# A two-layer diffusion backbone: when weight bounds are taken, and three stretches of the context's feed-forward in a written order

## The chip, the cores and the metric

The kernel runs on one core of a Trainium2 chip. The metric is the device time of one execution in microseconds (us), as the median of several runs. The core's engines are TensorE (PE, matrix products; its weight loads are listed as PEld), VectorE (DVE), ScalarE (ACT) and GpSimd (POOL); SyncE (SP) and POOL issue most of the transfers (DMA) between memory and the on-chip buffers. Each engine works through its own queue of instructions in the order in which they were put there.

## The reference

Two layers work on 1024 latent tokens and 256 context tokens of width 1024. Layer 0 mixes with Fourier groups and a Hyena convolution, layer 1 with neighbourhood attention; each ends with a SwiGLU feed-forward of width 2816. Cut to what the change touches:

```python
def rms_norm(x, g):
    y = x32 * lax.rsqrt(jnp.mean(x32 * x32, axis=-1, keepdims=True) + RMS_EPS)
    return (y * g).astype(x.dtype)
...
h_lat = h_lat + g1 * y_lat                                   # y = mixer(...) @ w_out
h_lat = h_lat + g2 * swiglu(modulate(rms_norm(h_lat, norm2_g[i]), sh2, sc2), w_gate, w_up, w_down)
if not last:
    h_ctx = h_ctx + cg1 * y_ctx
    h_ctx = h_ctx + cg2 * swiglu(modulate(rms_norm(h_ctx, norm2_g[i]), csh2, csc2), w_gate, w_up, w_down)
```

`swiglu(u)` is `(silu(u @ w_gate) * (u @ w_up)) @ w_down`, and `modulate` is `h * (1 + scale) + shift`. Layer 1 needs the context's result only as keys and values, so layer 0 is the only one with a feed-forward for the context.

## The kernel before

**Numbers.** Activations stand transposed: channels on the 128 partitions, tokens along the rows. `pc` names a part of the tokens: 0 and 1 are the two halves of the latent tokens (512 each), 2 is the context (256). Channels come in `KB = 8` blocks of 128, the feed-forward's width in `NFB = 22`. Each operand is split in a high and a low part (`split`: a copy on ACT, L301, and a difference on DVE, L303), and each product is three matmuls: high by high, high by low, low by high. `lin` makes the 24 matmuls of one output block over eight input blocks.

**Order.** The program is traced in the order of the text, and a scheduler then puts each engine's instructions in a queue, by their priority (their place in the text) and by a timing model. `follow` binds an instruction behind another one of its engine. Inside a `manual_schedule` region the named engines keep the order of the text instead; where the region's instructions fall among others stays the scheduler's choice. Before the change such regions exist in the attention and at the start of layer 1's feed-forward.

**The stages that the change touches, in order of time.**

- `out_proj` (L1192): the output projection of layer 0, in two groups of eight blocks: first `pc` 2 and 0 together, then `pc` 1. Each block's weight is split one block ahead. After a product DVE adds it to the residual (L1211), ACT squares the result (L510) and DVE adds up the squares (L515). One step of `qkv_sums` runs in each block.
- `qkv_sums` (L1269): 44 tiles of layer 1's and layer 0's weights (512 KB each, loaded from POOL's queue) are read for bounds of their size: ACT takes the absolute values and sums them (`abs_sums`, L1266). A step is three tiles.
- `after1` (L2362, in `run`), after each group: it stores the residual; after the first group it also computes the norm of the two parts. `rms_begin` sums the squares over the partitions on PE (one column per 128 tokens) and takes the root on ACT; `rms_end` scales an identity on ACT (L539), spreads it on PE, and ACT copies it back. `norm_block` makes the context's operand `uf`, `operand_scale` and `first_scales` the scales, and `wino_first` the upper half's operands for the latent product. After the second group only the norm of `pc` 1 is computed.
- `ffn` (L1515) with `l = 0`: for each of 22 blocks it loads and splits a gate and an up weight (`pair3`: three pairs of buffers in turn), makes the two products for the context, applies Silu on ACT (L1553), multiplies on DVE (L1554) and stores the hidden rows. From the third block on, each block also makes one of the 20 steps of `wino_second`: scaled operands (L1372), differences (L1378), a cast on ACT (L1363) and a low part on DVE (L1364).
- The latent gate and up follow as Strassen-like products (`wino_steps`, L1463): seven products for each pair of blocks, with `snap` (L1478) copying an accumulator out on ACT. `fetch(i, m)` loads and prepares the weights of pair `i`; for all but the first pair of a layer it first takes their bound with `abs_sums`.
- `down` (L1668): seven passes for the latent tokens, then (L1778 to L1810) the context's down product: 22 blocks of 24 matmuls into four accumulators. The splits of the weights use two pairs of buffers (`pair1`). `after(1)` (that is `after2` in `run`, L2384) normalizes `pc` 1 for layer 1 with `norm_half` (L569 on DVE, L571 on ACT, L572 on DVE) while it runs, at the calls of `hook`.
- Layer 1 begins with `values`. `halves_ahead` prepares layer-1 weights (L1232 on ACT, L1233 on DVE); the scheduler may put it into gaps of the context's down product.

Of the kernel before, what the change touches and what calls it, by code (L numbers as in the profile page):

```python
# [19 lines left out]
P = 128  # L20
# [181 lines left out]
class Builder:  # L202
# [359 lines left out]
    def norm_half(self, x, b, pc, act, r, cols):  # L562

        nc = self.nc
        w = WID[pc]
        cols = cols[1 if pc == 2 else 0]
        sh, sc = cols[:, b:b + 1], cols[:, 8 + b:9 + b]
        t = self.T()
        nc.vector.scalar_tensor_tensor(t[:, :w], x, sc, r[:, :w], op0=MUL, op1=MUL)  # L569
        hi, lo = act.ap(0, b, pc), act.ap(1, b, pc)  # L570
        nc.scalar.activation(hi, t[:, :w], AF.Identity, bias=sh)  # L571
        nc.vector.scalar_tensor_tensor(lo, t[:, :w], sh, hi, op0=ADD, op1=SUB)  # L572
# [619 lines left out]
    def out_proj(self, wname, y, groups, h, l, m, after, fill):  # L1192
        nc, a = self.nc, self.a
        todo = [nb for pcs in groups for nb in range(KB)]
        ready = []

        def fetch():
            if todo:
                ready.append(self.weights(a[wname][todo.pop(0)]))

        fetch()
        for pcs in groups:
            for nb in range(KB):
                wh, wl = ready.pop(0)
                fetch()
                acc = self.lin(wh, wl, 0, range(KB), y, pcs)
                next(fill, None)
                for pc in pcs:
                    w = WID[pc]
                    t = h.ap(0, nb, pc)  # L1210
                    nc.vector.scalar_tensor_tensor(t, acc[pc][:, :w], self.ada_col(l, pc, m, nb), t, op0=MUL, op1=ADD)  # L1211
                    self.square(t, nb, pc)
            after(pcs)
# [55 lines left out]
    def qkv_sums(self):  # L1269
# [7 lines left out]
        for j, k in enumerate((32, 33, 34, 35, *range(32), *range(36, 44))):  # L1277
# [3 lines left out]
            if j % 3 == 2:  # L1281
                yield
        yield
# [68 lines left out]
    def wino_second(self, h, l, m, r):  # L1352
# [8 lines left out]
        def out(key, j, src):  # L1361
# [3 lines left out]
            if l == 0 or len(late) > 1:  # L1365
                late.pop(0)()
# [96 lines left out]
    def wino_steps(self, w, tile, ctile=None):  # L1463
# [12 lines left out]
        def snap(ps, tile=tile):  # L1476
            t = tile()
            nc.scalar.copy(t, ps)  # L1478
            return t
# [35 lines left out]
    def ffn(self, l, u, h, hs, second, after, keep=None, begun={}):  # L1515
# [28 lines left out]
        if u is not None:  # L1544
            for fb in range(NFB):
                wide = 3 if fb < NFB - 2 else 2
                gh, gl = self.weights(a["gate"][l, fb], wide=wide)
                uh, ul = self.weights(a["up"][l, fb], wide=wide)
                lo = self.last_lo
                ga = self.lin(gh, gl, 0, range(KB), u, (2,))[2]  # L1550
                ua = self.lin(uh, ul, 0, range(KB), u, (2,))[2]
                t = self.T()
                nc.scalar.activation(t[:, :256], ga[:, :256], AF.Silu)  # L1553
                nc.vector.tensor_tensor(t[:, :256], ua[:, :256], t[:, :256], MUL)  # L1554
                self.ldr(hidc[fb // 2][:, fb % 2], t[:, :256])
                if fb >= 2:
                    with self.follow(last):
                        next(second, None)
                last = lo
# [31 lines left out]
        for i in range(n2):  # L1591
# [29 lines left out]
            if i or not begun:  # L1621
                fetch(i + 1, 0)
            g.to(5)
            up.to(1)
# [43 lines left out]
    def down(self, l, scales, bops, sops, hidc, hs, h, todo, after, keep):  # L1668
# [109 lines left out]
        if l == 0:  # L1778
# [4 lines left out]
            for kb in range(NFB):  # L1783
                hook(kb)
                if kb in (4, 8, 12, 16):
                    load_h((kb // 2 - 2, kb // 2 - 1), 2)
                t = self.S2(F32R)
                f = t[:, 256:].bitcast(F32)
                with self.follow(self.last_ldr):
                    self.ldr(f, hidc[kb // 2][:, kb % 2])  # L1790
                self.split(f, t[:, :256], t[:, 256:])
                f = self.pw.tile([P, 1024], F32, tag="ws", name=self.nm("ws")) if kb % 3 < 2 else self.S4()
                wh, wl = self.pair1()
                self.ld(f.rearrange("p (r k) -> p r k", r=2), w[kb].rearrange("r p k -> p r k"))
                self.split(f, wh, wl)
                for nb in range(KB):

                    o = acc[nb // 2][:, nb % 2 * 256:nb % 2 * 256 + 256]
                    with self.follow(end):
# [4 lines left out]
                    end = m.ins  # L1804
# [396 lines left out]
    def run(self):  # L2201
# [158 lines left out]
        rest = []  # L2360

        def after1(pcs):  # L2362
            spill(h, hs0, pcs)
            if 0 in pcs:
                uf.t.update(self.new_act(pcs=(2,)).t)
                rs = self.rms(pcs)
                for b in range(KB):
                    self.norm_block({b: h.ap(0, b, 2)}, b, 2, 0, 3, uf, rs[0])
                load_h((1,))
                self.ucol, self.usi = self.operand_scale(0, 3, (0, 1))  # L2370
                self.first_scales(0)
                for _ in self.wino_first(h, 0, 3, rs[1]):
                    pass
            else:
                rest.append(self.rms((1,))[0])

        load_h((2, 0))
        self.out_proj("w_out", y, [(2, 0), (1,)], h, 0, 2, after1, self.qkv_sums())
# [5 lines left out]
        def after2(pc):  # L2384
# [3 lines left out]
            yield  # L2388
            for b in range(KB):
                if b % 2 == 0:  # L2390
                    self.new_half(u1, ((b, pc), (b + 1, pc)))
                self.norm_half(h3.ap(0, b, pc), b, pc, u1, r, self.u1col)
                if b % 2:
                    yield

        h3 = Act()
        self.ffn(0, uf, h3, hs0, (x for r in rest for x in self.wino_second(h, 0, 3, r)), after2, hd)
# [210 lines left out]
```

## Time and profile before

| | |
|---|---|
| median of 3 runs | 2876.33 us (2871.45 to 2881.31) |
| the profiled execution's own time | 2880.55 us |
| its span, first to last instruction | 2878.8 us |
| mean granted clock of PE | 0.981 |
| output projection, first group | products from 722.3 to 789.9 us |
| second group | 796.0 to 843.2 |
| context's gate and up | 848.9 to 978.6 |
| context's down (but 12 products at 1587) | 1600.7 to 1668.8 |

The page of the profile gives, for each engine, the busy time over the span; the windows give the same for any stretch, with PEclk, the clock that the throttle granted to PE, as a share of full speed. The timeline lists instructions in order; a bracket holds the idle time in front of one and what ended it. A group of instructions has its count, busy time and mean duration. Matmuls overlap, so the pace of a row of products is read from their starts, not from their durations.

### The profile page before, as it was taken

What the parts mean: (1) busy time and instruction counts of PE and PEld (TensorE: products, weight loads), DVE (VectorE), ACT (ScalarE), POOL (GpSimd) and SP (SyncE); (2) the same over time, 40 slices, a digit from 0 to 9 for tenths busy, and PEclk for the clock granted to TensorE, in tenths of its full rate; (3) what the DMA queues carried; (4) which work ended last, traced back from release to release, by engine and by line L of the source; (5) the groups of instructions that cost most, each with busy time, mean ns of one, the idle gap of its engine ahead of it and who ended that gap; (6) DMA issues with size and microseconds to landing.
All of it is one profiled execution on the core that took longest, in us unless ns stands there. A gap on an engine that the chain in (4) does not pass through costs nothing. (4 is left out here: it accounts for less than half of the span.)

```text
span 2878.8 us, 46360 instructions
## 1 busy us (share of the span) xinstructions
PE 2751.2 (96%) x16419; PEld 1684.7 (59%) x16419; DVE 2082.7 (72%) x3857; ACT 1620.5 (56%) x2857; POOL 594.4 (21%) x977
## 2 busy tenths in 40 slices
PE   6989999999999999999999899999999999999998
PEld 3766556878879744444455754666665444444554
DVE  4778867585367798886886877777775788775755
ACT  4674324454575666664555555666663486564543
POOL 1012013264220111122111112333431022102001
PEclk8899999999999999999999999999999999999999
DMA  7574435358785655565996599778775676425653
GB/s 257 190 263 164 167 119 156 104 177 262 288 330 211 216 211 198 198 208 191 330 323 242 206 345 347 173 167 177 162 201 174 231 262 226 146 92 187 225 198 122
DMA packets 323363, 607.60 MB, mean 211 GB/s; under 512 B 89910, under 2 KB 131576, under 8 KB 323130
## 3 DMA queue, kind: packets, MB, share of 16 engines
q1 hardware_dynamic: 254682, 387.53, 42.0%
q0 software_dynamic: 66144, 212.91, 21.0%
q10 hardware_dynamic: 2304, 4.20, 0.4%
q8 instruction: 129, 2.11, 0.3%
q14 instruction: 104, 0.85, 0.1%
HBM read 455.33 MB, written 135.53 MB: 205 GB/s over the span
## 5 line engine op out<-in xcount | busy, mean ns | idle before, releaser
L1473 PE MATMUL ps<-s,s 128*128 128x512 f16 x2244 | 506.1, 381 | 9.5 <-ACT g L1478 5.2
L1473 PEld LDWEIGHTS <-s 128*128 128x128 f16 x2640 | 257.9, 98 | 324.8 <-issue 18.0
L297 PE MATMUL ps<-s,wh 128*128 128x256 f32 (+3 forms) x1716 | 387.0, 329 | 11.1 <-ACT wh L301 5.4
L1232 ACT ACTIVATE s<-s,c 128x512 f16<-128x512 f32 (+1 forms) x324 | 233.1, 752 | 151.5 <-DMA s<-d 86.9
L1233 DVE SCALAR_TENSOR_TENSOR s<-s,c,s 128x512 f16<-128x512 f32 (+1 forms) x324 | 248.2, 793 | 91.8 <-ACT s L1232 91.2
L1698 PE MATMUL ps<-s 128*128 128x512 f16 (+2 forms) x1308 | 303.6, 378 | 2.0 <-DVE s L1233 2.0
L297 PE MATMUL pq<-s,wh 128*128 128x512 f16 (+1 forms) x940 | 259.2, 352 | 2.0 <-ACT wh L1232 1.7
L297 PE MATMUL ps<-s,wl 128*128 128x256 f32 (+3 forms) x858 | 254.6, 330 | 1.3 <-DVE wl L303 1.2
L1698 PEld LDWEIGHTS <-s 128*128 128x128 f16 x1536 | 148.4, 98 | 179.0 <-issue 6.8
L297 PEld LDWEIGHTS <-wh 128*128 128x128 f16 x1568 | 149.8, 99 | 138.1 <-issue 12.5
L288 POOL DMA_DIRECT2D d<-s x201 | 109.1, 543 | 580.5 <-DVE s L1233 159.8
L349 ACT CAST mat<-cs 128x1024 fp32r<-128x1024 f16 (+2 forms) x120 | 111.6, 935 | 140.1 <-PE ps L297 55.9
L297 PEld LDWEIGHTS ps<-s,wh 128*128 128x128 f32 x1088 | 177.7, 192 | 18.1 <-ACT wh L301 5.7
L297 PE MATMUL ps<-s,mat 128*128 128x512 f32 x696 | 180.9, 406 | 4.7 <-DVE s L303 4.4
L1473 PE MATMUL ps<-s,wh 128*128 128x512 f16 x608 | 182.4, 379 | 1.6 <-DVE g L1487 1.2
L297 PE MATMUL pq<-s,wl 128*128 128x512 f16 (+1 forms) x470 | 162.9, 352 | 0.0
L297 PEld LDWEIGHTS <-s 128*128 128x128 f16 x2400 | 113.4, 98 | 80.0 <-issue 10.2
L297 PEld LDWEIGHTS ps<-s,mat 128*128 128x128 f32 x696 | 133.6, 194 | 39.0 <-DVE s L303 5.6
L1266 ACT ACTIVATE t<-s 128x1024 bf16<-128x1024 f32 (+1 forms) x164 | 141.3, 863 | 12.1 <-DVE c L484 8.6
L297 PE MATMUL sc<-s,s 128*128 128x65 f16 (+3 forms) x2688 | 143.2, 231 | 3.3 <-ACT t L2106 2.4
L1232 ACT ACTIVATE s<-t,c 128x512 f16<-128x512 f32 x172 | 115.3, 711 | 22.6 <-DVE c L1333 9.3
L1233 DVE SCALAR_TENSOR_TENSOR s<-t,c,s 128x512 f16<-128x512 f32 x172 | 123.4, 745 | 1.6 <-ACT s L1232 1.6
(438 smaller groups left out, 5504.6 us busy)
## 6 DMA issues: line engine op xcount, KB each, us to landing
s<-d SPq DMA_DIRECT2D x294, 256.0 KB, 4.3
d<-s POOLq DMA_DIRECT2D x157, 256.0 KB, 3.2
s<-in_down SPq DMA_DIRECT2D x154, 256.0 KB, 4.9
s<-in_ada_w POOLq DMA_DIRECT2D x48, 512.0 KB, 4.9
s<-in_gate SPq DMA_DIRECT2D x46, 512.0 KB, 3.8
s<-in_up SPq DMA_DIRECT2D x46, 512.0 KB, 4.2
d<-g POOLq DMA_DIRECT2D x87, 256.0 KB, 3.2
d<-tk POOLq DMA_DIRECT2D x82, 256.0 KB, 4.7
```

The source lines that it names most:

```text
L288: self.last_ldr = self.nc.gpsimd.dma_start(out, in_).ins
L297: return self.nc.tensor.matmul(o, l, r, start=st, stop=sp).ins
L349: self.nc.scalar.copy(m, st)
L1232: nc.scalar.activation(hi, src, AF.Copy, scale=scale)
L1233: nc.vector.scalar_tensor_tensor(lo, src, scale, hi, op0=MUL, op1=SUB)
L1266: self.nc.scalar.activation(junk[:, :t.shape[1]], t, AF.Abs, scale=2.0 ** -15, accum_out=st[:, k:k + 1])
L1473: nc.tensor.matmul(ps, x[:, sl], y, start=first and j == 0 and x is wh and y is xh, stop=j == 3 and x is wl, skip_group_check=True)
L1698: m = nc.tensor.matmul(acc[j][:, c0:c1], x[:, sl], y[:, xs], start=first and k == 0, stop=last and k == 2, skip_group_check=True)
```

## The change

The bounds (`qkv_sums`) take one tile a step instead of three. In the first group of `out_proj` each block runs three steps, in the second one, and 12 of the 44 tiles are left for `ffn`, one in each block from the third on. The norm of the first group moves from the boundary between the groups to behind the first product of the second group (`norm1`). The norm of `pc` 1 and the first scales move into `ffn` (`second1`). The gate and up loop and the context's down loop of `ffn` and `down` are written out with loads ahead (four weights there, two here), splits ahead (two products, one block) and a `manual_schedule` region for PE, ACT and DVE. `fetch(1, 0)` moves behind the fifth step of the first latent gate product, and its bound behind the last `snap`. In `wino_second` a low part is always made one step after its cast. For `pc` 1 `after2` scales on ACT and multiplies by the norm on GpSimd, and the rest of `norm_half` follows one step later.

```diff
     def out_proj(self, wname, y, groups, h, l, m, after, norm, fill):
...
-        for pcs in groups:
+        for g, pcs in enumerate(groups):
             for nb in range(KB):
                 wh, wl = ready.pop(0)
                 fetch()
                 acc = self.lin(wh, wl, 0, range(KB), y, pcs)
-                next(fill, None)
+                if g and nb == 0:
+                    norm(groups[g - 1])
+                for _ in range(1 if g else 3):
+                    next(fill, None)
...
             self.abs_sums([t], self.qs[:, k:k + 1])
-            if j % 3 == 2:
-                yield
-        yield
+            yield
...
             late.append(lambda: nc.vector.tensor_tensor(lo, src, hi, SUB))
-            if l == 0 or len(late) > 1:
+            if len(late) > 1:
                 late.pop(0)()
...
+            def part(k):
+                stage(k + 4)
+                if k < 2 * NFB:
+                    ready[k] = self.pair3() if k // 2 < NFB - 2 else self.pair1()
+                    self.split(staged.pop(k), *ready[k])
+
+            def hidden(fb):
+                ga, ua, t = pending.pop(fb)
                 nc.vector.tensor_tensor(t[:, :256], ua[:, :256], t[:, :256], MUL)
                 self.ldr(hidc[fb // 2][:, fb % 2], t[:, :256])
...
+            with self.tc.manual_schedule(engines={e.PE, e.Activation, e.DVE}):
+                part(0)
+                part(1)
+                for fb in range(NFB):
+                    ga = self.lin(*ready.pop(2 * fb), 0, range(KB), u, (2,))[2]
+                    if fb == 0:
+                        next(second)
+                    else:
+                        hidden(fb - 1)
+                    part(2 * fb + 2)
+                    ua = self.lin(*ready.pop(2 * fb + 1), 0, range(KB), u, (2,))[2]
+                    if fb == 0:
+                        next(second)
+                    t = self.T()
+                    nc.scalar.activation(t[:, :256], ga[:, :256], AF.Silu)
+                    pending[fb] = ga, ua, t
+                    if fb >= 2:
                         next(second, None)
-                last = lo
+                        next(fill, None)
+                    part(2 * fb + 3)
+                hidden(NFB - 1)
...
-            if i or not begun:
+            if i:
                 fetch(i + 1, 0)
             g.to(5)
+            if i == 0 and not begun:
+                self.behind = self.last_snap
+                fetch(1, 0)
             up.to(1)
...
+            def part(kb):
+                stage(kb + 2)
+                if kb < NFB:
+                    t, f, x = staged.pop(kb)
+                    ready[kb] = t, *self.pair1()
+                    self.split(x, *ready[kb][1:])
+                    self.split(f, t[:, :256], t[:, 256:])
...
+            with self.tc.manual_schedule(engines={e.PE, e.Activation, e.DVE}):
+                part(0)
+                for kb in range(NFB):
+                    part(kb + 1)
+                    t, wh, wl = ready.pop(kb)
+                    for nb in range(KB):
...
+                    if kb % 2 or kb == 2:
+                        next(done, None)
...
+        def second1():
+            c = self.rms_begin(1)
+            yield
+            r = self.rms_end(1, c)
+            yield
+            self.first_scales(0)
+            yield from self.wino_second(h, 0, 3, r)
...
+                if pc == 1:
+                    t = self.T()
+                    nc.scalar.mul(t, h3.ap(0, b, pc), self.u1col[0][:, 8 + b:9 + b])
+                    nc.gpsimd.tensor_tensor(t, t, r, MUL)
+                    late.append((t, b))
+                    if b:
+                        self.shift_half(*late.pop(0), pc, u1, self.u1col)
+                    yield
+                    continue
```

More of the change, by code (lines that the diff above doesn't have):

```diff
@@ L1189, in fourier_c, with out_proj @@
             self.split(raws[g][:, :256], y.ap(0, g, 2), y.ap(1, g, 2))
-    def out_proj(self, wname, y, groups, h, l, m, after, fill):
+    def out_proj(self, wname, y, groups, h, l, m, after, norm, fill):
         nc, a = self.nc, self.a
@@ L1513, in wino_begin, with ffn @@
         return s
-    def ffn(self, l, u, h, hs, second, after, keep=None, begun={}):
+    def ffn(self, l, u, h, hs, second, after, keep=None, begun={}, fill=()):
         nc, a = self.nc, self.a
@@ L1544, in ffn @@
         if u is not None:
[L1545 to L1553, printed above, removed]
+            staged, ready, pending = {}, {}, {}
@@ L1555, in ffn @@
                 self.ldr(hidc[fb // 2][:, fb % 2], t[:, :256])
-                if fb >= 2:
-                    with self.follow(last):
-                        next(second, None)
-                last = lo
+            for k in range(4):
+                stage(k)
+            e = mybir.EngineType
+            with self.tc.manual_schedule(engines={e.PE, e.Activation, e.DVE}):
[15 more added lines that the diff above has]
+                    if fb >= 2:
+                        next(second, None)
+                        next(fill, None)
+                    part(2 * fb + 3)
+                hidden(NFB - 1)
@@ L1560, in ffn @@
+            for _ in fill:
+                pass
             self.load_cond()
@@ L1782, in down, with stage @@
             acc = [self.PP() for _ in range(4)]
[L1783 to L1799, printed above, removed]
+            staged, ready = {}, {}
+            def stage(kb):
+                if kb < NFB:
+                    if kb in (4, 8, 12, 16):
+                        load_h((kb // 2 - 2, kb // 2 - 1), 2)
+                    t = self.S2(F32R)
+                    f = t[:, 256:].bitcast(F32)
+                    with self.follow(self.last_ldr):
+                        self.ldr(f, hidc[kb // 2][:, kb % 2])
+                    x = self.pw.tile([P, 1024], F32, tag="ws", name=self.nm("ws")) if kb % 3 < 2 else self.S4()
+                    self.ld(x.rearrange("p (r k) -> p r k", r=2), w[kb].rearrange("r p k -> p r k"))
+                    staged[kb] = t, f, x
+            def part(kb):
+                stage(kb + 2)
+                if kb < NFB:
+                    t, f, x = staged.pop(kb)
+                    ready[kb] = t, *self.pair1()
+                    self.split(x, *ready[kb][1:])
+                    self.split(f, t[:, :256], t[:, 256:])
+            stage(0)
+            stage(1)
+            e = mybir.EngineType
+            with self.tc.manual_schedule(engines={e.PE, e.Activation, e.DVE}):
[4 more added lines that the diff above has]
+                    for nb in range(KB):
+                        o = acc[nb // 2][:, nb % 2 * 256:nb % 2 * 256 + 256]
                         for k, (x, c) in enumerate(((wh, 0), (wh, 256), (wl, 0))):
@@ L2364, in after1, with norm1 @@
             if 0 in pcs:
[L2365 to L2368, printed above, removed]
                 load_h((1,))
[L2370 to L2375, printed above, removed]
+        def norm1(pcs):
+            uf.t.update(self.new_act(pcs=(2,)).t)
+            rs = self.rms(pcs)
+            for b in range(KB):
+                self.norm_block({b: h.ap(0, b, 2)}, b, 2, 0, 3, uf, rs[0])
+            self.ucol, self.usi = self.operand_scale(0, 3, (0, 1))
+            for _ in self.wino_first(h, 0, 3, rs[1]):
+                pass
+        def second1():
[5 more added lines that the diff above has]
+            yield from self.wino_second(h, 0, 3, r)
         load_h((2, 0))
[L2378 removed]
+        sums = self.qkv_sums()
+        self.out_proj("w_out", y, [(2, 0), (1,)], h, 0, 2, after1, norm1, sums)
         for b in range(8):
@@ L2394, in after2 @@
                     yield
+            for t, b in late:
+                self.shift_half(t, b, pc, u1, self.u1col)
+                yield
         h3 = Act()
-        self.ffn(0, uf, h3, hs0, (x for r in rest for x in self.wino_second(h, 0, 3, r)), after2, hd)
+        self.ffn(0, uf, h3, hs0, second1(), after2, hd, fill=sums)
         for b in range(8):
```

15 lines of the change are left out of this document (12 added, 3 removed).

## The prediction

> **What bounds the kernel now.** I read the page first, then windows of 10 us, then TensorE's (PE's) timeline for the rows that carry an idle time.
>
> ```profile
> PE 2751.2 (96%) x16419; PEld 1684.7 (59%) x16419; DVE 2082.7 (72%) x3857; ACT 1620.5 (56%) x2857; POOL 594.4 (21%) x977
> ```
>
> PE is the bound: it is busy for 96% of the span, so 4%, some 115 us, are idle in all. The change can win only the part of it in its own stages, and what a low clock costs there. Windows; the columns are the stretch, its length, the busy times of PE, PEld, DVE, ACT and POOL, then PEclk, DMA share and GB/s:
>
> ```profile
> 790.00:800.00 10.00, 7.61 (x26) 6.44 (x27) 6.62 (x19) 7.33 (x17) 1.08 (x2) 0.66 0.76 256
> ...
> 840.00:850.00 10.00, 5.08 (x24) 3.76 (x23) 2.80 (x4) 7.21 (x15) 2.19 (x4) 0.85 1.03 419
> ...
> 870.00:880.00 10.00, 6.97 (x44) 6.77 (x45) 8.50 (x11) 5.75 (x8) 0.54 (x1) 0.83 0.76 273
> 880.00:890.00 10.00, 10.00 (x90) 10.00 (x90) 8.26 (x13) 5.87 (x8) 1.08 (x2) 1.00 0.43 142
> ```
>
> There are holes at 790 and from 840 to 880, where the granted clock is 0.66 to 0.85, and a steady stretch from 880 on. Two more places are the seam at 990 and the context's down product after 1600. PE's timeline at the first three:
>
> ```profile
> 789.41 0.50 PE L297 MATMUL ps<-s,wl 128*128 128x256 f32 x2
> 792.39 2.66 PE L297 MATMUL pq<-c,tk 128*128 128x1 f32 x12 [2.48 <-DVE tk L515]
> 794.91 1.20 PE L297 MATMUL pq<-t,c 128*128 128x256 f32 x2
> ...
> 795.98 1.20 PE L297 MATMUL ps<-s,wh 128*128 128x512 f32 x2
> ...
> 799.67 0.64 PE L297 MATMUL ps<-s,wh 128*128 128x512 f32 x2
> ...
> 806.12 0.63 PE L297 MATMUL ps<-s,wh 128*128 128x512 f32 x2
> ...
> 806.82 0.62 PE L297 MATMUL ps<-s,wh 128*128 128x512 f32 x2
> ...
> 845.47 1.05 PE L297 MATMUL pq<-c,tk 128*128 128x1 f32 x8 [2.23 <-DVE tk L515]
> 848.85 0.79 PE L297 MATMUL ps<-s,wh 128*128 128x256 f32 x2 [2.32 <-ACT wh L301]
> ...
> 872.27 0.51 PE L297 MATMUL ps<-s,wh 128*128 128x256 f32 x2 [3.07 <-ACT wh L301]
> ...
> 976.06 0.39 PE L297 MATMUL ps<-s,wh 128*128 128x256 f32 x2
> ...
> 976.40 0.39 PE L297 MATMUL ps<-s,wh 128*128 128x256 f32 x2
> ...
> 978.32 0.28 PE L297 MATMUL ps<-s,wl 128*128 128x256 f32 x1
> ...
> 990.92 4.20 PE L1473 MATMUL ps<-s,s 128*128 128x512 f16 x12 [2.86 <-ACT g L1478]
> ```
>
> The reader is to see who is late. At 792 and 845 PE stands before the norm's column sums, which need the last square (DVE L515). At 848 and 872 it stands before a weight's high half (ACT L301), at 990 before an eviction (ACT L1478). Two paces serve below: three 512-wide products start every 806.82 - 806.12 = 0.70 us, and three 256-wide ones every 976.40 - 976.06 = 0.34 us, so 24 of these, one block of gate, up or down, take 2.72 us.
>
> **1. Sums a block later.** Between the end of the first group (789.41 + 0.50 = 789.91) and 795.98 lie 6.1 us. The column sums and the spread of the inverse root stay PE's work wherever they stand: 12 at the pace of the 8 that took 1.05 is 1.6 us, the spread some 0.6. Removed are 6.1 - 2.2 = 3.9 us, because 24 products of the next block now stand first and the squares are done behind them; that block's weights were split a block ahead. From 795.98 to 799.67 nine products took 3.7 us instead of 2.1, at the low clock; with no hole this 1.6 goes too. Together 5.5. Behind the moved step eight normalized context blocks and the upper half's operands start 5 us later, under some 40 us of products that cover them. I take **-5** (bounds 0 and -5.5).
>
> **2. The context's gate and up in a written order.** Here is where it may cost as much as it wins. The stretch of before runs from the end of the second group, where DVE's L1211 stops waiting, to 978.6:
>
> ```profile
> 843.27 0.75 DVE L1211 SCALAR_TENSOR_TENSOR s<-ps,c,s 128x512 f32<-128x512 f32 x1 [3.41 <-PE ps L297]
> ```
>
> That is 135.4 us. PE's work in it is 44 x 2.72 = 119.7, plus about 2 for the sums and the spread: 121.7. So 13.7 us are lost now, all of it before 880. Part of the cause is ACT, which takes weight bounds (L1266) between the splits. The change leaves 12 of the 44 bounds for this loop, one in each of blocks 2 to 13, splits two products ahead, and puts the second norm after the first gate product. The loads keep their queues: the weights on SP, four ahead, the bounds' tiles on POOL, now among the stores of the hidden rows; rival (c) prices a late one. The holes at 845 and 848 should close. But now ACT and DVE issue strictly in the order of the text. Durations (groups by form of 722 to 990, and one row of DVE's timeline):
>
> ```profile
> L303 DVE TENSOR_TENSOR wl<-s,wh 128x1024 fp32r<-128x1024 f32 x44 | 53.7, 1225 | 31.8 <-ACT wh L301 31.8
> ...
> L1266 ACT ACTIVATE t<-s 128x1024 bf16<-128x1024 f32 x45 | 47.0, 1044 | 1.7 <-DMA s<-in_gate 1.7
> L301 ACT CAST wh<-s 128x1024 fp32r<-128x1024 f32 x44 | 45.8, 1048 | 39.6 <-issue 26.3 <-PE ps L297 13.1
> ...
> L1363 ACT CAST s<-s 128x512 f16<-128x512 f32 x16 | 9.9, 616 | 6.4 <-DVE s L1378 5.3 <-DVE s L1386 0.9
> L1554 DVE TENSOR_TENSOR t<-ps,t 128x256 f32<-128x256 f32 x22 | 9.2, 420 | 5.0 <-ACT t L1553 4.4 <-PE ps L297 0.6
> ...
> L1372 DVE SCALAR_TENSOR_TENSOR s<-s,c,t 128x512 f32<-128x512 f32 x8 | 5.9, 747 | 1.8 <-ACT t L543 1.8
> ...
> L1378 DVE TENSOR_TENSOR s<-s,s 128x512 f32<-128x512 f32 x4 | 2.7, 683 | 0.0
> ```
> ```profile
> 852.58 2.36 DVE L303 TENSOR_TENSOR wl<-s,wh 128x1024 fp32r<-128x1024 f32 x2 [2.53 <-ACT wh L301]
> ```
>
> Follow one block, from ACT's cast of an up weight to the next block's: cast 1.05; on DVE the low half 1.23, the hidden product 0.42, the next low half 1.23, the scaled operand 0.75 and the difference 0.68; back on ACT the operand's cast 0.62 and the bound 1.04. The sum is 7.0 us. Rows back to back overlap by about 0.09 (two low halves in 2.36, not 2.45), which makes it 6.7. PE wants a block every 5.44. Behind the waiting operand cast stand, on ACT, the bound and the next weight's cast, and PE waits for that weight. So 1.25 us a block are lost in the eight blocks whose step has both DVE operations (2 to 9), and about 0.6 in the four with one (10 to 13): 10 + 2.4. The start adds two waits. In block 0 ACT does the root, the four scalings, a copy and a table load before the weight of block 1: 1.6. In block 2 the first bounds' reduction passes through PE, so DVE's step begins only when the up product ends, and the next up weight is some 3 late. Total 17 us lost, against 13.7 now: **+3**. Without the bounds the cycle is 5.7 us, and some 7 are lost: -7. If nothing but the start's 4.6 remains: -9. If each wait is half as long again: +11.
>
> The table load has a row:
>
> ```profile
> 863.36 1.28 ACT L1553 ACT_TABLE_LOAD   x1
> 864.65 0.66 ACT L1553 ACTIVATE t<-ps 128x256 f32<-128x256 f32 x2
> ```
>
> It takes 1.28 us, and the activation follows at its end; I use that. The Trainium skill (ScalarE: Activation LUTs, What ACT_TABLE_LOAD costs) adds a drain of about 1.38 us to each switch; by it block 0 would lose up to 2.8 more, and the part would be +6. This trace shows no such gap before 864.65.
>
> **3. The seam to the latent gate.** Before 990.92 PE idles 2.86 us, and the 12 products take 4.20 us, where twelve at 0.70 for three take 2.8: together 4.3. The eviction it waits for stood behind bounds of the next gate block, which the change issues after that eviction. Two bounds of 1.04 us go from in front; operand splits stay there. I take **-3** (0 to -4.3). The bound itself is needed only a block later, behind some ten products of 12 matmuls, so I cost its delay at nothing.
>
> **4. The context's down in a written order, the norm partly on GpSimd.** PE's timeline, and groups by form of 1600 to 1664:
>
> ```profile
> 1591.85 2.86 PE L1698 MATMUL ps<-s 128*128 128x512 f16 x12 [1.97 <-DVE s L1233]
> ...
> 1600.71 0.51 PE L1801 MATMUL ps<-s,wh 128*128 128x256 f32 x2 [0.89 <-DVE s L1719]
> ```
> ```profile
> 1627.02 0.38 PE L1801 MATMUL ps<-s,wl 128*128 128x256 f32 x1 [2.11 <-DVE wl L303]
> ```
> ```profile
> L1801 PE MATMUL ps<-s,wl x176: 276/276/391, 1587.7 to 1668.5; 128*128 128x256 f32 x176
> ```
> ```profile
> L569 DVE SCALAR_TENSOR_TENSOR t<-s,c,t 128x512 f32<-128x512 f32 x8 | 5.6, 747 | 0.0
> ```
> ```profile
> L915 POOL TENSOR_TENSOR t<-t,t 128x512 f32<-128x512 f32 x40 | 53.7, 1360 | 70.0 <-DVE t L914 68.2 <-ACT s L301 1.3
> ```
>
> From 1600.71 to 1668.8 are 68.1 us. PE's work is 22 x 2.72 = 59.8, less 1.4 for 12 products that ran at 1587, plus 2: 60.4. So 7.7 are lost, the longest wait of 2.11 where eight normalizations ran in a bunch on DVE. The change takes 8 x 0.75 = 6 us off DVE, puts 8 x 0.7 on ACT and 8 x 1.36 on GpSimd, and spreads the norm over every second block. But only two weight buffers exist: when a block ends, cast 1.05, low half 1.23 and the hidden's low half (0.42, now issued behind it) must fit in the 2.72 of the other block. They sum to 2.70, so any hold shows. I expect half of the loss to stay, and about 1 us to go from the 1.97 before 1591.85, since the hidden's splits no longer run there ahead of time: **-4.5** (bounds -8 and +2).
>
> GpSimd can hold DVE up. In the timeline of 585 to 590 one form, a 256-wide product on DVE (L990), runs once beside GpSimd and once alone:
>
> ```profile
> 585.38 1.17 POOL L988 TENSOR_TENSOR t<-t 128x256 f32<-128x256 f32 x1 [0.33 <-DVE t L987]
> ...
> 585.88 0.94 DVE L990 SCALAR_TENSOR_TENSOR t<-t,c,s 128x256 f32<-128x256 f32 x1
> ...
> 589.83 0.47 DVE L990 SCALAR_TENSOR_TENSOR t<-t,c,s 128x256 f32<-128x256 f32 x1
> ```
>
> The hold is 0.47 us; eight of them are 3.8, which are in the half that stays. The Trainium skill (GPSIMD Engine Reference, 1. Specifications) says that GpSimd shares its SBUF interface with VectorE and that DVE instructions with two SBUF inputs contend. By that rule each low half that meets a GpSimd product is held; the trace agrees here.
>
> **Sum.** -5 + 3 - 3 - 4.5 = -9.5. The layer-1 halves that filled gaps of the down product move into the next stage, +0.5: **-9 us**. The profiled execution took 2880.55 us (span 2878.8), 4.2 above the median of 2876.33 (runs 2871.45 to 2881.31). I subtract from the median: **2867 us**.
>
> **Rivals.** (a) The bounds hide in ACT's waits, and only the start is lost in part 2 (-9 instead of +3): -21, 2855. For it: ACT and DVE are both under 70% busy there. Against: the cycle above is latency, not load. 0.18. (b) The written down product is as slow as before, each chain of 2.70 us held by GpSimd or by layer-1 splits put between, and part 4 gives nothing, or the first weights of gate are queued behind the last square (0.75 + 0.63 + 1.05 + 1.23 us, so it is the same to the end): -5, 2871. 0.25. (c) Slower: a bound in ACT's queue waits for its tile. Tiles of this path have landed late:
>
> ```profile
> DMA to landing us min/median/max: 3.1/7.6/13.7
> ```
>
> (that is w_out's). If the buffers leave one tile in flight, its load starts when the last bound ends, and the next is wanted 5.7 us later; at 7.6 each waits 2, 12 of them 24: +15, 2891. It decides from a landing of 5.7 us on. Against: DMA share is 0.43 from 880 on, and w_out's buffers are free by then. 0.10. The forecast has 0.47, and its own range is 2861 to 2873.
>
> **Chances.** A measurement of this kernel can tell about 0.3%, 8.6 us, from no change, so "faster" begins at 2867.7. It gets (a) and rather more than half of the forecast, 0.45; "same" the rest of the forecast and (b), 0.45; "slower" (c), 0.10. The range 2852 to 2881 leaves out (c) and the far end of (a).
>
> **What would show it.** Step 1: no wait for L515 between the groups, PEclk 1.00. Step 2: from some 860 to 930 PE waits of about 1.2 us for L303 in every up product, twelve of them, and one of 3 us in front; it is wrong if the stretch is steady, or if the waits name a DMA. Step 3: no wait over 1 us for L1478. Step 4: the products of L1801 within 64 us, the waits short and even; wrong if ACT's or DVE's splits of layer 1 stand before them. A time under 2857 says that part 2 is mis-sized, one over 2880 that the written order binds throughout.

## The result, and the profile after

The changed kernel takes **2922.6 us** (median of 4 runs, 2915.5 to 2926.79) against 2877.39 for the kernel before beside it: a ratio of 1.0151, interval 1.0130 to 1.0172. It is 1.5% slower; 2867 was forecast.

The page of the changed kernel, engine line first:

```profile
PE 2762.4 (95%) x16419; PEld 1690.7 (58%) x16419; DVE 2086.5 (72%) x3849; ACT 1625.1 (56%) x2865; POOL 607.1 (21%) x985
```

PE has the same 16419 instructions and 11 us more busy time, at a mean granted clock of 0.979 instead of 0.981; the span grew by 34.9 (2878.8 to 2913.7), so most of the loss is idle time. By stage, from the end of one stage's last product to the end of the next's (values: to the first product of the attention's scores), us:

| stage | before | after | forecast for the difference |
|---|---|---|---|
| output projection, from its first product | 120.9 | 115.6 | -5 |
| context's gate and up | 135.4 | 161.4 | +3 |
| latent gate and up | 420.0 | 421.0 | -3 |
| latent down | 201.2 | 202.5 | 0 |
| context's down | 68.9 | 76.0 | -4.5 |
| values, up to the scores | 131.8 | 143.2 | +0.5 |
| all behind it | 1078.2 | 1077.7 | 0 |

As rounded, these differences sum to +41.0; the changed kernel's execution reached the output projection 6.0 us earlier, in code that both share and that moved between 716.3 and 725.9 in other executions too. Three stages hold the loss. The first, windows of the changed kernel; columns as in the prediction:

```profile
832.00:994.00 162.00, 135.92 (x1072) 130.91 (x1071) 91.51 (x119) 87.95 (x135) 19.03 (x35) 0.95 0.63 220
```

And PE's waits in it (who waited for whom: us in total, times, longest):

```profile
PE ps L297 <- ACT wh L301: 16.3, 7, 4.6
PE ps L297 <- DVE wl L303: 6.5, 9, 0.8
PE pq L297 <- ACT t L539: 3.3, 1, 3.3
```

The forecast's short waits for DVE are there (9 of 0.7). Above them stand seven for ACT, up to 4.6 us long. What ACT did, in its timeline, then POOL's and PE's:

```profile
876.63 1.06 ACT L1276 ACTIVATE t<-s 128x1024 bf16<-128x1024 f32 x1 [4.62 <-DMA s<-in_w_out]
877.59 0.19 ACT L1276 ACTIVATION_READ_ACCUMULATOR t<-s 128x1 f32 x1
877.68 1.98 ACT L301 CAST wh<-s 128x1024 fp32r<-128x1024 f32 x2
```
```profile
869.13 0.55 POOL L288 DMA_DIRECT2D d<-t  x1 [6.21 <-DVE t L1568]
869.74 1.09 POOL L288 DMA_DIRECT2D s<-in_w_out  x2
```
```profile
878.76 0.79 PE L297 MATMUL ps<-s,wh 128*128 128x256 f32 x2 [4.61 <-ACT wh L301]
```

Read them from the bottom. PE waits for a weight's high half. That cast stands on ACT behind a bound (L1276), which waits 4.62 us for its tile. The tile's load was issued at 869.74, because POOL's queue had stood 6.21 us at a hidden row's store, which waits for DVE's product (L1568). Then two loads leave together. Five of the twelve bounds find their tile late (ACT's waits, over the whole stretch):

```profile
ACT t L1276 <- DMA s<-in_gate: 7.3, 2, 4.1
...
ACT t L1276 <- DMA s<-in_up: 5.5, 2, 4.2
ACT t L1276 <- DMA s<-in_w_out: 4.6, 1, 4.6
```

With the order written out nothing passes such a bound on ACT.

The context's down, PE's waits, and DVE's timeline beside POOL's:

```profile
PE ps L1856 <- DVE s L303: 7.8, 9, 1.4
```
```profile
1639.66 1.50 DVE L303 TENSOR_TENSOR s<-s 128x256 fp32r<-128x256 f32 x1
...
1642.88 0.41 DVE L303 TENSOR_TENSOR s<-s 128x256 fp32r<-128x256 f32 x1
```
```profile
1639.49 1.39 POOL L2459 TENSOR_TENSOR t<-t,t 128x512 f32<-128x512 f32 x1 [5.25 <-ACT t L2458]
```

The hidden row's low half takes 1.50 us beside a GpSimd product and 0.41 alone: it ends 0.28 us after the product does (so in all eight cases), and PE waits for it.

In the values stage PE's waits name an eviction by ACT (L1976) and a key's split on DVE:

```profile
PE pq L297 <- ACT tk L1976: 7.9, 1, 7.9
...
PE pq L297 <- DVE s L303: 1.7, 1, 1.7
```

### The profile page after: what moved, and what is told of

It is laid out like the page before. It is cut to its first block, busy times and chain, and to the rows that moved or that the text cites. A ratio compares the mean times of both kernels' runs of the same rounds, so it can differ in the third digit from the quotient of the medians.

```text
span 2913.7 us, 46352 instructions
## 1 busy us (share of the span) xinstructions
PE 2762.4 (95%) x16419; PEld 1690.7 (58%) x16419; DVE 2086.5 (72%) x3849; ACT 1625.1 (56%) x2865; POOL 607.1 (21%) x985
## 5 line engine op out<-in xcount | busy, mean ns | idle before, releaser
L1276 ACT ACTIVATE t<-s 128x1024 bf16<-128x1024 f32 (+1 forms) x164 | 141.4, 863 | 28.5 <-DVE c L484 9.4
```

Source lines behind the costliest of these rows:

```text
L1276: self.nc.scalar.activation(junk[:, :t.shape[1]], t, AF.Abs, scale=2.0 ** -15, accum_out=st[:, k:k + 1])
```

## The experiments

Unless said otherwise each starts from the changed kernel. "Written order" is the `manual_schedule` block; without it the order of the three engines is the planner's.

### The context's gate and up

**No written order in the gate loop.**

```diff
-            with self.tc.manual_schedule(engines={e.PE, e.Activation, e.DVE}):
+            with nullcontext():
                 part(0)
                 part(1)
```

> The changed kernel, with the written order of the gate and up loop taken away (the scheduler orders PE, ACT and DVE there); the bounds stay in the loop. In the changed kernel the stretch from the last product of the second group to the last gate product takes 161.4 us against 135.4 before, and PE's own work in it is 121.7. Theory W (the written order makes PE wait: an operand's cast, then a bound that waits for its tile, stand on ACT in front of a weight's cast): the stretch falls to 128 to 142 us and the time by 20 to 33 us. Rival L (the bounds as such are too much, in any order): it stays over 150 us and the time falls by under 10.

Measured: 2878.9 us, ratio to the kernel before 1.0002 (0.9988 to 1.0017); the time fell by more than the 20 to 33 us expected. The gate stretch takes 129.6 instead of 161.4, and PE runs it at full clock:

```profile
836.00:966.00 130.00, 124.25 (x1071) 122.02 (x1070) 91.85 (x119) 88.22 (x136) 18.89 (x35) 1.00 0.78 276
```

The written order of this loop costs about as much as the whole result. (The profiled execution of the changed kernel was the fastest of its runs; three other kernels with the same loop took 165.6 to 168.5 for the stretch, so that 32 is the low end.) With the same bounds and splits in the planner's order, the stretch is even 5.8 us shorter than before.

**All bounds before the loop.**

```diff
-                for _ in range(1 if g else 3):
+                for _ in range(3):
                     next(fill, None)
```

> The changed kernel, with three bounds in each block of the second group too, so that none of the 44 is left for the gate loop; the written order stays. Theory W: with no bound in the loop what is left is the start and the shorter cycle, 5 to 8 us lost, so the stretch takes 127 to 131 us (30 less), and the second group grows by at most 4 us. Rival O (the order is late even without bounds, by the operand casts and the hidden products): the stretch stays over 142 us.

Measured: 2915.24 us, 1.0128 (1.0102 to 1.0154). The stretch is 159.4, hardly less. Its windows say where:

```profile
841.00:880.00 39.00, 10.90 (x62) 9.33 (x62) 5.39 (x7) 22.36 (x42) 5.41 (x11) 0.66 1.02 413
880.00:1000.00 120.00, 117.67 (x1006) 115.76 (x1006) 86.69 (x112) 64.78 (x90) 11.92 (x22) 1.00 0.53 177
```

The bounds' tiles now crowd the stretch up to 880: DMA share 1.02, 413 GB/s, and PE stands 8.7 and 19.0 us while ACT works through bounds and waits for their tiles. From 880 on, where no bound is left, the same written order keeps PE busy for 117.67 of 120 us. The expected 127 to 131 us failed, and by its own limit of 142 us rival O would hold; but the windows put the loss ahead of 880, among the bounds, and not into the order: that alone costs little.

**The late bounds' loads on SP's queue.**

```diff
-            self.ldr(t, src[k])
+            (self.ld if j >= 32 else self.ldr)(t, src[k])
```

> The changed kernel, with the twelve tiles of the gate loop's bounds loaded from SP's queue instead of POOL's, where their loads stand behind stores of hidden rows; written order and bounds stay. Theory Q (half of the loss is a bound that waits 3 to 5 us for a tile whose load stands behind a store on POOL, in six of the twelve blocks): no wait of ACT's bounds for a DMA is left, the stretch falls from 161 to 140 to 148 us and the time by 13 to 20. Rival C (the chain of casts on ACT alone makes the loss): it falls by under 6.

Measured: 2902.8 us, 1.0085 (1.0059 to 1.0110); the stretch 143.4, 18 less. ACT's waits for bounds' tiles are gone, and of PE's waits stay

```profile
PE ps L297 <- DVE wl L303: 7.1, 12, 0.8
PE pq L297 <- ACT t L539: 3.3, 1, 3.3
PE ps L297 <- ACT wh L301: 1.7, 1, 1.7
```

Twelve waits for DVE, one a bound: the chain of ACT and DVE that the forecast worked out, at 0.6 us each, where it had 1.25 for eight of them and 0.6 for four.

**The written order without any bound in it.**

```diff
                         next(second, None)
-                        next(fill, None)
                     part(2 * fb + 3)
```

> The kernel after, with the written order kept in the gate loop, but none of the twelve bounds in it: they are issued behind the loop. The gate stretch (end of the second group's products to gate's last product) is 135.4 us before, 161.4 after, 129.6 with no written order, 143.4 with the bounds' tiles loaded ahead on SP's queue. Theory W (what costs is that ACT stands before a bound whose tile is late): 127 to 137 us, some 25 less, of which up to 12 come back behind the loop, 12 bounds of 1.04 us: 2895 to 2908. Theory O (the order's own cycle of ACT and DVE costs without any bound): 148 us or more, time 2910 or more.

Measured: 2903.84 us, 1.0082 (1.0066 to 1.0098); the stretch 134.7, theory W's range. The twelve bounds come back behind it: the latent gate and up takes 436.6 instead of 421.0. So of the 161.4 - 129.6 = 32 us that the written order costs here, about 18 are tiles behind the stores on POOL's queue (161.4 to 143.4), some 9 are the bounds as such (143.4 to 134.7), and 5 are the order with none of the twelve in it. In that kernel PE has one long wait left, of 5.2 us for the spread of the norm (ACT L539): on ACT three bounds of the output projection, one of them waiting 1.8 us for its tile, stand between the root and that step.

### The context's down

**The products on DVE instead of GpSimd.**

```diff
-                    nc.gpsimd.tensor_tensor(t, t, r, MUL)
+                    nc.vector.tensor_tensor(t, t, r, MUL)
```

> The changed kernel, with the eight multiplications of the norm of pc 1 on DVE instead of GpSimd; order and places stay. In the changed kernel the context's down takes 76.0 us from the end of the latent passes (69.0 before), with eight waits of 0.87 us for a hidden row's low half that took 1.50 us beside a GpSimd product instead of 0.42. Theory P (GpSimd holds DVE for its whole product): the waits of 0.87 go, down takes 66 to 69 us, the time falls by 7 to 10, and by up to 20 if the 7.9 us wait at the end of the values stage goes too. Rival D (the two-buffer chain is the bound whoever multiplies): down stays at 73 or more.

**No written order in the down loop**, alone and together with the gate loop's:

```diff
-            with self.tc.manual_schedule(engines={e.PE, e.Activation, e.DVE}):
+            with nullcontext():
                 part(0)
                 for kb in range(NFB):
```

> The kernel after, without the written order in the context's down loop; all else stays. In the two kernels the context's down takes 69.0 us before and 76.0 after, the values stage behind it 131.8 and 143.2. Theory D: the written order does both: it keeps layer 1's halves out of the down loop (first one 33.7 us into it before, 64.5 after) and so pushes their traffic into the values stage. Then the down takes 68 to 70, the values 131 to 134, and the time is 18 us below after: about 2904. Rival G: GpSimd's products hold DVE whatever the order, and the values stage is longer for another reason: down 73 to 76, values 141 to 144, time 2918 to 2923.

> The kernel after, without either written order (gate loop, context's down loop). With the gate loop free alone it took 2878.9 us. Theory D (the down's written order costs the down 7 and the values stage 11 us): 18 less, 2858 to 2864, faster than before. Rival G (the GpSimd products cost it): 2874 to 2880, as before.

Measured: products on DVE 2913.29 us, 1.0128 (1.0095 to 1.0161); down free 2913.24 us, 1.0115 (1.0098 to 1.0133); both free 2877.11 us, 0.9987 (0.9974 to 1.0000). The down stage answers each:

| context's down, us | products on GpSimd | on DVE |
|---|---|---|
| written order | 73.1 to 76.0 (six kernels) | 68.4 |
| planner's order | 68.2 to 70.3 (four kernels) | 65.3 |

(65.3 is one kernel, of the next part, whose norm has its old form. The kernel before, with the old loop and the old norm, has 68.9. The times alone don't decide it: with the products on DVE the interval overlaps with that of the changed kernel, 2913.24 lies between the two theories, and 2877.11 in rival G's range.) Groups by form in the down stage, changed kernel and then with the products on DVE:

```profile
L303 DVE TENSOR_TENSOR s<-s 128x256 fp32r<-128x256 f32 x20 | 17.0, 850 | 0.0
```
```profile
L303 DVE TENSOR_TENSOR s<-s 128x256 fp32r<-128x256 f32 x20 | 8.4, 418 | 0.0
...
L2459 DVE TENSOR_TENSOR t<-t,t 128x512 f32<-128x512 f32 x8 | 5.5, 684 | 0.0
```

DVE does 5.5 us of products more and is done earlier: its low halves fall by 17.0 - 8.4 = 8.6 us, and PE's waits for them from 7.8 to 0.6. In the planner's order the hold costs some 3 to 5 us (68.2 to 70.3 against 65.3) instead of 5 to 8. Both theories held for this stage, each in part. For the values stage theory D failed: with the down free, layer 1's halves enter the down loop again (the first 37 us into it, 64 in the changed kernel), yet the values take 141.5 and 142.4, not 131 to 134.

### The values stage

**Eight stores fewer.**

```diff
-                d = self.halves[(n, b)] = self.DR([P, 2048], F16)
-                self.ldr(d, t)
+                if n == "wk":
+                    d = self.DR([P, 2048], F16)
+                    self.ldr(d, t)
+                self.halves[(n, b)] = d
```

This kernel leaves out the stores of wq's halves and reads wk's in their place, so it computes something else than the others.

> The kernel after, leaving out 8 stores of 512 KB in the values stage (wq's layer-1 halves are split, but not stored; wk's are read in their place). The two kernels' values stages move 46.3 MB in 134.0 us and 50.5 MB in 145.0 us, with a DMA share of 0.94 and 0.95. Theory T (the values stage is bound by transfers, and the displaced halves are 4.2 MB more): 4.2 MB at 348 GB/s are 12 us, values 130 to 134 us instead of 143.2, time about 2911. Rival S (the displaced splits on ACT and DVE stand in front of the values' evictions; transfers are hidden): values 141 to 145, time 2920 to 2925.

Measured: 2919.03 us, 1.0127 (1.0107 to 1.0148); values 137.9, between the two. Transfers are part of it, not all. What remains shows in the kernel with both orders free, at the end of this stage. PE's timeline, DVE's, POOL's, and POOL's instructions of one line:

```profile
1782.46 1.01 PE L297 MATMUL pq<-s,wh 128*128 128x512 f16 x2 [5.01 <-DVE s L303]
```
```profile
1774.53 0.17 DVE L1982 TENSOR_REDUCE c<-c 128x1 f32<-128x20 f32 x1
1781.08 0.15 DVE L1984 TENSOR_SCALAR c<-c 128x1 f32<-128x1 f32 x1 [6.38 <-POOL c L1983]
...
1781.72 0.68 DVE L303 TENSOR_TENSOR s<-pq,s 128x512 fp32r<-128x512 f32 x1
```
```profile
1773.66 0.27 POOL L2056 MEMSET s<- 128x8 f16 x4
1780.67 0.38 POOL L1983 PARTITION_ALL_REDUCE c<-c  x1 [6.75 <-issue]
```
```profile
L1983 POOLq MODIFY_POOL_CONFIG  x2: 37/37/37, 1774.1 to 1774.1; - x2
```

PE waits for a key's low half, which is queued on DVE behind the values' scale, which waits for the maximum over partitions on POOL. POOL has its input at 1774.7 and starts at 1780.67. At 1774.1 its sequencer shows MODIFY_POOL_CONFIG, and then nothing for 6.6 us; this idle time of POOL is called the stand below. In the kernel before, the same line has no such instruction, and POOL waits 0.87:

```profile
1787.65 0.35 POOL L1926 PARTITION_ALL_REDUCE c<-c  x1 [0.87 <-DVE c L1925]
```

There the last GpSimd work with arithmetic was also a maximum over partitions; in the changed kernel it was a product of the norm.

**Both orders free, and the norm in its old form** (no ACT scaling, no GpSimd product):

```diff
-                if pc == 1:
-                    t = self.T()
-                    nc.scalar.mul(t, h3.ap(0, b, pc), self.u1col[0][:, 8 + b:9 + b])
-                    nc.gpsimd.tensor_tensor(t, t, r, MUL)
...
-                    continue
```

> The kernel after, without either written order and with the context's norm in its old form (no GpSimd product, no ACT scaling). The values stage is 131.8 us before; it is 142.4 with both orders free (PE idle 10.8 in it, 5.0 of it 130 us in), 147.2 with the norm on DVE but a written down loop (one idle stretch of 9.8 us at 118). With GpSimd products in the norm, POOL stands 6.0 to 6.8 us before the maximum over partitions that ends the stage, with no releaser in the profile; without them 0.9 to 1.5. Theory L: that stand is the price of going back from a GpSimd product to the maximum, and the rest of the growth is the halves that the written down loop pushes back. Here both are gone: values 131 to 135, down 68 to 70, gate 127 to 131, time 2864 to 2871. Rival N (the values stage is longer for a third reason, common to all the changed kernels): values 140 to 145, time 2875 to 2881.

Measured: **2862.26 us**, 0.9943 (0.9929 to 0.9957): faster than both kernels by more than their uncertainty. Values 133.0 and gate 128.1 are as expected; the down stage, 65.3, is below the 68 to 70 expected. POOL waits 0.88 before the maximum.

**The change of work on GpSimd by itself.** Two kernels were meant to move the stand or to make one, with a dummy instruction.

```diff
+        d1, d2 = self.C(1), self.C(1)
+        nc.vector.memset(d1, 1.0)
...
+                if tbs[0] == 4 and ch == 0:
+                    nc.gpsimd.partition_all_reduce(d2, d1, channels=P, reduce_op=bass.bass_isa.ReduceOp.max)
```

(for the kernel before, with `nc.gpsimd.tensor_tensor(d2, d1, d1, MUL)` instead)

> Both orders free, GpSimd products kept, and a maximum over partitions of a dummy column added some 40 us ahead of the one that ends the values stage. Theory L: the stand of 6 to 7 us moves in front of the dummy, where only stores wait for POOL; in front of the real one 0.5 to 1.5 stay, and the values stage falls from 142.4 to 136 to 139, the time from 2877 to 2871 to 2874, though there is one instruction more. Rival N (the stand belongs to this place, not to the instruction before it): 6 us in front of both, values 141 to 145, time 2876 to 2881.

> The kernel before, with one GpSimd product of 128x1 numbers added some 40 us ahead of the maximum that ends the values stage. Theory L: POOL then stands 6 to 7 us in front of the maximum (0.9 in the kernel before), the values stage grows from 131.8 to 136 to 138, and the time is 4 to 6 us over before: 2882 to 2886. Rival N: no stand over 2 us, values 131 to 133, time as before.

They gave 2874.21 us (0.9985, 0.9975 to 0.9995) and 2879.96 (1.0008, 0.9999 to 1.0017), and tell nothing: the dummies depend on nothing late, and the planner put them at 16.2 and 4.9 us of the kernel. With an input from the stage itself, `mx[:, 10:11]` for `d1`, they stay in place:

> Both orders free, GpSimd products kept, one maximum over partitions added that reads a value of the second quarter of the values stage, so that it can't run before some 40 us into it (the dummy of the run before ran at 16 us of the kernel, before anything it was to separate). Theory L: a stand of 5 to 7 us in front of the added one, 0.5 to 1.5 in front of the one that ends the stage (6.75 without it), the idle stretch of PE at 130 us (5.0) gone, values 134 to 138 instead of 142.4, time 2868 to 2873. Rival N: 5 us or more in front of both, values 140 to 144, time 2875 to 2880.

> The kernel before, with one GpSimd product of 128x1 numbers added in the values stage that reads a value of its second quarter, so that it lies between the last two maxima over partitions. Theory L: POOL stands 6 to 7 us in front of the maximum that ends the stage (0.9 before), the values stage grows from 131.8 to 135 to 138, time 4 to 6 us over before, 2881 to 2885. Rival N: no stand over 2 us, values 130 to 133, time as before.

Measured: 2867.6 us (0.9961, 0.9947 to 0.9975) and 2885.96 (1.0026, 1.0015 to 1.0036); values 135.2 and 141.7. POOL's timeline of the first, then of the second:

```profile
1708.44 0.38 POOL L1976 PARTITION_ALL_REDUCE c<-c  x1 [8.48 <-DVE c L1980]
...
1778.39 0.35 POOL L1986 PARTITION_ALL_REDUCE c<-c  x1 [0.89 <-DVE c L1985]
```
```profile
1717.95 0.18 POOL L1919 TENSOR_TENSOR c<-c 128x1 f32<-128x1 f32 x1 [6.86 <-issue]
...
1791.67 0.38 POOL L1929 PARTITION_ALL_REDUCE c<-c  x1 [6.75 <-issue]
```

An added instruction makes the kernel with both orders free faster, by some 7 us (0.9961 against 0.9987 without it), as it takes the stand at an idle moment. And one product of 128 numbers, 0.18 us long, makes the kernel before slower by 0.26%, about 7 us, with PE's same wait of 5.0 us behind it. Theory L is shown. The values of the second grew by 9.9, where 3 to 6 were expected; a part of the rest is the clock, which is low in the 10 us in which that wait ends:

```profile
1790.00:1800.00 10.00, 6.55 (x17) 2.31 (x17) 2.28 (x8) 0.72 (x1) 2.12 (x5) 0.66 0.73 181
```

At 0.66 these 10 us give 3.4 less; the kernel before has 1.00 to the end of the stage.

The other part goes with the written down loop. With products on DVE there is no stand, yet the values take 147.2 with that loop written and 133.0 with it free. (The norm's form and the gate loop's order differ too; the down loop's order alone, with the old norm, was not run.) There one wait of 9.8 us is left, for an eviction that ACT takes behind splits of layer 1's halves, whose tiles come late in a stage at a DMA share of 0.94:

```profile
1806.16 1.15 ACT L1242 ACTIVATE s<-s,c 128x1024 f16<-128x1024 f32 x1 [3.98 <-DMA s<-in_up]
...
1817.29 0.56 ACT L1976 COPY tk<-pq 128x512 f32<-128x512 f32 x1
```

What the stage moves fits this. Windows of the kernel before, of both orders free with the old norm, and of the written orders with products on DVE:

```profile
1669.00:1800.00 131.00, 128.09 (x604) 59.04 (x603) 96.28 (x138) 71.47 (x101) 24.20 (x50) 1.00 0.95 348
```
```profile
1645.00:1778.00 133.00, 129.29 (x610) 59.46 (x608) 99.23 (x143) 74.49 (x106) 24.11 (x50) 1.00 0.94 345
```
```profile
1700.00:1848.00 148.00, 133.68 (x618) 60.94 (x617) 102.94 (x146) 77.60 (x109) 26.72 (x55) 0.95 0.94 344
```

The rate is the same, 344 to 348 GB/s, so the stage's length follows its bytes: 45.6 MB, 45.9 MB and 50.9 MB. The 5 MB more, at that rate, are some 14 us. With both orders free and products on GpSimd the rate falls to 328 GB/s (46.9 MB in 143 us): there the stand adds time in which less is moved. So the halves cost up to 14 us, the stand 5 to 10 (139.8 to 142.4 with both orders free, against 133.0 and 135.2 where nothing waits for it; 9.9 in the kernel before), and both together no more than the halves alone (the stage takes 143 to 147): with the halves pushed back the transfers set the length, and the stand hides behind them. That the one hides the other is inferred from these sizes.

## Why the prediction was wrong

**Step 1 was right**: -5 forecast, 5.3 measured, the same in every kernel with the change (115.6 against 120.9). Its sign came true too: no wait for L515, and a clock of 1.00 over the whole projection.

**Step 2 failed, by 23 us**, at the sentence "The loads keep their queues: the weights on SP, four ahead, the bounds' tiles on POOL, now among the stores of the hidden rows". The cycle was summed as if the tile were there. Rival (c), a bound that waits for its tile in ACT's queue, named this wait, with a price of 24 and a chance of 0.10, but another cause (slow landing, one tile in flight); the argument against it, a DMA share of 0.43, was about the wrong thing. The tiles are late because their issue stands behind a store that waits for DVE, not because transfers are slow: the share is 0.63 in the stretch, and the same loads from SP's queue leave no such wait. The prediction's own sign, "or if the waits name a DMA", came true one step away: PE's waits name ACT, and ACT's name the DMA. The chain of ACT and DVE is there, smaller than priced: 12 waits, 7.1 us instead of 12.4, once the tiles come in time.

The sum had a second gap: the 17 us lost were waits alone, set against 13.7 lost before, of which only 8.8 are waits (2.2, 5.4 and 1.2); the rest goes with a clock of 0.96. In the changed kernel the waits are 26.1 (16.3 + 6.5 + 3.3), but 161.4 - 121.7 = 39.7 are lost; the other 13.6 are products that take longer, with the clock at 0.95 over the stretch, and the sum put them at nothing. (With the loop free, at 1.00, only 2.1 are lost beside 5.8 of waits.) So "Without the bounds ... -7" measured -0.7 (134.7 against 135.4), though PE's waits there, 7.1, are about what was forecast.

**Step 3 failed**: the stage took 421.0 instead of 420.0, where -3 was forecast. The long wait of the seam moved to another product: 2.86 us before 990.92 became

```profile
1032.04 4.17 PE L1481 MATMUL ps<-s,s 128*128 128x512 f16 x12 [3.40 <-ACT tk L1486]
```

In front of that eviction ACT again takes splits and bounds:

```profile
1029.78 1.04 ACT L1276 ACTIVATE t<-s 128x1024 bf16<-128x1024 f32 x1
...
1031.43 0.56 ACT L1486 COPY tk<-ps 128x512 f32<-128x512 f32 x1
```

The term that failed is "so I cost its delay at nothing": PE's idle time in the stage is 10.3 us instead of 10.0. Whether these are the moved bounds, or others that they pushed, is not shown. Over the kernels without added bounds the stage lies between 417.3 and 421.5 with 9.5 to 11.2 us idle in each; what differs is the clock (1.00 where it takes 417.3, 0.99 in the kernel before and the changed one).

**Step 4 failed in its size**: -4.5 forecast (bounds -8 and +2), +7.1 measured, and +4.2 to +7.1 over the six kernels with this loop and norm. That a chain of 2.70 in 2.72 us lets "any hold" show was right. The hold was taken as 0.47 us, from a DVE product that began 0.50 us into a GpSimd product of 1.17 and ended 0.27 after it; here the low half begins 0.17 into one of 1.39, and the hold is 1.50 - 0.41 = 1.09 for each of eight. The written order lets nothing fill it. With no hold it took 68.4, only 0.5 under the kernel before, so the half of the loss that was to go did not go either.

**"+0.5" for the displaced halves failed, by 11**: they cost up to 14 in a stage that transfers fill, and the change of GpSimd's work, priced nowhere, 5 to 10 where they don't. The trace of before had it. Its instructions of the other maxima over partitions:

```profile
L1252 POOLq MODIFY_POOL_CONFIG  x6: 8/37/37, 47.3 to 1253.0; - x6
...
  issue: 11.9, 2
```

These are two stands of some 6 us; the fourth of these maxima, at 1476.1, follows another maximum and has no such instruction.

What was read there were the durations of GpSimd's products, not what comes between two kinds of its work.

**Rival (a)**, only the start is lost in the gate loop, is nearly what the planner's order does: the stretch is 127.8 to 129.6 instead of 135.4. With the orders free and the old norm the sum is -5.3 (step 1) - 7.3 (gate) - 2.0 (latent gate) - 3.6 (down) + 1.2 (values), -17.0 us; the time fell by 15.5.

Two numbers of the prediction are off, and nothing hangs on them: PE's idle time before is 127.6 us (2878.8 less 2751.2), not "some 115", and waits half as long again would be +12, not +11.

## What to carry to other kernels

A written order makes every wait of its slowest member a wait of all behind it, so ask of each instruction in it not only how long it is, but through which queue its input comes and behind what that queue stands; keep work with uncertain inputs out of it. An engine with time to spare isn't free: price what it does to its neighbour's operands and what it pays to change its kind of work. And where a stage has transfers at their limit, work pushed into it costs its full transfer time.

## What the runs showed of the hardware

- GpSimd pays for going from products to a maximum over partitions and back: some 6 us between MODIFY_POOL_CONFIG and the first instruction (1826.0 to 1831.87 in the changed kernel, 1774.1 to 1780.67 with both orders free; on the way back the added product of 0.18 us waited 6.86), marked "issue" in the timeline, with nothing busy on POOL. The Trainium skill (GPSIMD Engine Reference, 2.1 Instruction dispatch) gives about 6 us for the first call of a freshly loaded kernel, from MODIFY_POOL_CONFIG on and with no visible instruction; these traces agree in the size. That it is paid again at each change of kind is what the runs here show.
- The two-input DVE instructions here that meet a GpSimd product aren't slowed by a share but held to the product's end: 0.41 becomes 1.50 beside a product of 1.39, 0.28 of it behind the product. In the planner's order the products are slower as well, on average 1945 ns instead of 1371 (groups of the down stage, changed kernel, then both orders free):

```profile
L2459 POOL TENSOR_TENSOR t<-t,t 128x512 f32<-128x512 f32 x8 | 11.0, 1371 | 59.8 <-ACT t L2458 54.5 <-issue 5.3
```
```profile
L2459 POOL TENSOR_TENSOR t<-t,t 128x512 f32<-128x512 f32 x8 | 15.3, 1945 | 24.6 <-ACT t L543 24.6
```
